# Two-layer hybrid mixer and mixture-of-experts kernel: normed rows stored from ScalarE's queue, routing reordered, one norm of four tiles between the layers

## The chip, the cores and the metric

The kernel runs on one core of one Trainium2 chip. The metric is the time of one execution on the device in microseconds (us); for a version it is the median of its runs. All times below are us unless marked otherwise. Engines are named TensorE (PE), VectorE (DVE), ScalarE (ACT), GpSimd (POOL) and SyncE (SP); SP does nothing but issue DMAs here.

## What is computed

Two layers, each a mixer of four kinds of heads and then a mixture of 16 experts with two experts per token, on 512 tokens of width 1024, all in fp32. Cut to what matters:

```python
for l in range(DEPTH):                                   # 2 layers
    sh1, sc1, g1, sh2, sc2, g2 = jnp.split(mod_all[l][:, None, :], 6, axis=-1)
    h = _rms_norm(x, norm_mix_g[l]) * (1.0 + sc1) + sh1
    proj = h @ w_in[l]
    ...
    mix = jnp.concatenate([y_nsa, y_pool, y_rwkv, y_dil], axis=-1).astype(x.dtype)
    x = x + g1 * (mix @ w_out[l])
    h2 = _rms_norm(x, norm_ffn_g[l]) * (1.0 + sc2) + sh2
    x = x + g2 * _moe(h2, router_w, router_b, moe_w_gate[l], moe_w_up[l], moe_w_down[l])

def _moe(h, router_w, router_b, w_gate, w_up, w_down):
    aff = jax.nn.sigmoid(jnp.einsum('bsd,de->bse', h, router_w).astype(F32))
    sel = (aff + router_b).reshape(B, S, N_EXPERT_GROUPS, EXPERTS_PER_GROUP)
    grp = jnp.argmax(jnp.sum(lax.top_k(sel, TOP_K)[0], axis=-1), axis=-1)
    ...                                                  # two experts of the best group, weights
    act = jax.nn.silu(hg) * hu * gates[..., None].astype(h.dtype)
    return jnp.einsum('bsef,efd->bsd', act, w_down)
```

## The kernel before

The 512 tokens are four tiles of 128 rows (`NT` = 4). Each layer goes through the same stages: the projection into the mixers (chunks of `w_in`, in the names `c` and `t`), the mixers themselves, the output projection `W_out`, the routing, and a loop over the 16 experts. Every large matmul is done as three (`mm3`, lines 616 to 618) on a high and a low part of each operand: ScalarE makes the high part of a weight (`wh`, line 568), VectorE the low part (`wl`, line 569). Weights come by DMAs of 512 KB that SP issues (line 585).

**What sets the order.** Each engine executes its instructions in the order in which they were emitted. The kernel emits them from Python generators: one main program and side streams, which `W.spawn` adds. At each `yield` a planner (`_Clock`, a model of every engine's time, and the weaver `W`) decides which stream emits next; it knows a cost for each instruction and the moment at which its data is ready by that model. A stream that yields a flag is resumed once the flag is done.

**The output projection and the routing** (lines 1836 to 2100). `W_out` is done in two halves of 512 columns. `evac(t, p_)` (line 1981) scales a tile of the result and adds it to `xt[t]` on VectorE, squares it on ScalarE (`jk`, line 1986), and for the second half writes x*A into `hs[t]` on GpSimd (line 1989) and spawns `norm(t)`. `half(t, q)` (line 1847) transposes four 128x128 blocks of tile t on TensorE (`tp`), copies them on ScalarE (`xT`, line 1853), multiplies them with the router (`lg`) and adds the result into `lgt`. `norm(t)` (line 1865) computes 1/rms of the rows (`rsl`) on VectorE, scales the tile, and stores it in DRAM as `h2d` (line 1884), from where the experts' rows are gathered later. By `NQ = "VVAV"` tile 2 is scaled on ScalarE with an addition on GpSimd, the others by two operations of 128x512 on VectorE (line 1882). After tile 2's store, `keep` (line 1888) stores the residual rows of tiles 0 to 2 (`xs_d`, or the output in the last layer) from ScalarE's queue (`XWQ` = 2).

`route` (line 1903) waits for all four tiles: logits times `rsl`, a tanh on ScalarE (`aff`, line 1911), scores (`sel`, `prs`), the best group (`gsc` and after), the two experts, and each token's rank within its expert (`rank`). `onehot(e)` (line 1895) writes eight one-hot matrices of 128x128 for experts e and e+1 on VectorE, `slots` (line 2048) turns them into row numbers (`idx`) by small matmuls on TensorE (`sps`), and `slot_weights` (line 2061) into the rows' weights (`wt`, by `swt`). `gather(e)` (line 2073) is an indirect DMA of GpSimd that brings an expert's rows out of `h2d`; `etrans(e)` transposes them on TensorE (`etp`), and ScalarE and VectorE split them (`eh`, `el`). Experts 0 to 3 get slots and weights ahead of the loop; those of experts 4 to 15 are a side stream, `more_slots` (line 2090), two experts per block.

**Between the layers** (lines 2291 to 2312) the four tiles are read back from `xs_d`; ScalarE squares them (`square`, line 822), and `normed_` normalises them by pairs (0, 1) and (2, 3), the even tile on ScalarE, the odd one on VectorE. Layer 1 then transposes the normed tiles (`tp`, line 906) in eight steps of `part_of` (line 912), each for 128 columns of all tiles: TensorE, then `hf`, `hH` and `hL` on ScalarE and VectorE. In layer 0 the upper four steps are a side stream for which `cchunk` waits at its third of four steps (line 984); in layer 1 all eight run first.

Of the kernel before, what the change touches and what calls it, by code (L numbers as in the profile page):

```python
# [36 lines left out]
ADG = ("c0","hdone","hdone")    # L37
ADL = 0  
ADE = "PPPPPPPP"
HWQ = 0  # L40
NQ = "VVAV"
SL = -1500  
PP = 1  
# [409 lines left out]
def fused(ctx: ExitStack, tc: tile.TileContext, A, out, dbg=None):  # L453
# [425 lines left out]
    def layer(l, xt, mixs, moes, nmixs):  # L879
# [32 lines left out]
        def part_of(ks, late=None):  # L912

            for k in ks:
                if l == 0:
                    src = f_ = hf[k // 2][:, k % 2]
                else:
                    src = transposed(k)
                    f_ = HG("hf1")
                if k % 2:  # L920
                    SC.activation(f_, src, AF.Identity, scale=A1[:, k:k + 1], bias=B1[:, k:k + 1])
                else:
                    V.tensor_scalar(f_, src, A1[:, k:k + 1], B1[:, k:k + 1], op0=OP.mult, op1=OP.add)
                SC.activation(parts[k][0], f_, AF.Copy)
                if late:
                    V.tensor_tensor(late[2], late[0], late[1].bitcast(F32), op=OP.subtract)  # L926
                late = (f_,) + parts[k]
                yield
            V.tensor_tensor(late[2], late[0], late[1].bitcast(F32), op=OP.subtract)

        upper = None
        if l == 0:
            def raise_(k):
                tp = transposed(k)
                if k % 2:
                    V.tensor_copy(hf[k // 2][:, k % 2], tp)
                else:
                    SC.activation(hf[k // 2][:, k % 2], tp, AF.Copy)

            def cols(jj):  # L940
                mcv = mcol(PB("mc"), 0, 4)
                hs_ = slice(4 * jj, 4 * jj + 4)
                V.scalar_tensor_tensor(A1[:, hs_], mcv[:, :, 2 + jj], 1.0, col("gmix", 4 * jj, 4), op0=OP.add, op1=OP.mult)
                V.tensor_copy(B1[:, hs_], mcv[:, :, jj])

            def upper_half():
                yield from ada_first(1)
                cols(1)
                yield
                yield from part_of(range(4, 8))  # L950

            ada_s.cap = 16
            ada_s.load(8)
            mixs.load(2)
            ada_s.load(12)
            mixs.load(3)
            ada_s.load(16)
            mixs.load(4)
            steps = ada_first(0)
            for _ in range(4):  # L960
                next(steps)
            for k in range(4):
                raise_(k)
            mixs.presplit(1)
            for _ in steps:
                pass
            cols(0)
            for k, _ in enumerate(part_of(range(4)), 4):
                raise_(k)
            upper = W.spawn(upper_half(), front=True, lead=0)  # L970
        else:
            for _ in part_of(range(8)):
                pass
        hH = [hH[k // 2][:, k % 2] for k in range(8)]
        hL = [hL[k // 2][:, k % 2] for k in range(8)]
        yield
# [865 lines left out]
        rank = lay.tile([128, 64], F32, name="rank")  # L1842
        mb = lay.tile([128, 64], BF, name="mb")
        hs = {}
        oh, hsides, normed = {}, {}, {}

        def half(t, q):

            xT_ = HG("xT")
            tp = PB("tp2")  # L1850
            for k in range(4):
                PE.transpose(tp[:, k * 128:(k + 1) * 128], xt[t][:, (4 * q + k) * 128:(4 * q + k + 1) * 128], ident)
            SC.activation(xT_, tp, AF.Copy)
            yield hsides.get((t, q - 1))
            lg = PB("lg")
            for k in range(4):
                PE.matmul(lg[:, 0:16], lhsT=xT_[:, k * 128:(k + 1) * 128], rhs=RP.rwa[:, 4 * q + k], start=k == 0,
                          stop=k == 3)
            ls_ = lgt[:, t * 16:(t + 1) * 16]
            if q:  # L1860
                V.tensor_tensor(ls_, ls_, lg[:, 0:16], op=OP.add)
            else:
                V.tensor_copy(ls_, lg[:, 0:16])

        def norm(t, after):

            ms, rs = TI("ms", 1), rsl[:, t:t + 1]
            V.tensor_scalar(ms, ms2[:, t, 0:1], ms2[:, t, 1:2], EPS, op0=OP.add, op1=OP.add)
            yield
            yield from rsqrt_cols(ms, rs, 1)  # L1870
            after.done, after.ready = True, K.mark
            if NQ[t] == "A":
                SC.activation(hs[t], hs[t], AF.Copy, scale=rs)
                yield
                for j in range(PP):
                    w_ = 1024 // PP
                    js = slice(j * w_, (j + 1) * w_)
                    GP.tensor_tensor(hs[t][:, js], hs[t][:, js], RP.B2.rearrange("p a b -> p (a b)")[:, js], op=OP.add)
            else:
                for j in range(2):  # L1880
                    js = slice(j * 512, (j + 1) * 512)
                    V.scalar_tensor_tensor(hs[t][:, js], hs[t][:, js], rs, RP.B2[:, j], op0=OP.mult, op1=OP.add)
                    yield
            HQ.dma_start(h2d[t * 128:(t + 1) * 128], hs[t])
            if XW == 0 and t == KP:
                keep(xt[:t + 1])
# [16 lines left out]
        def route():  # L1903
# [5 lines left out]
            yield  # L1909
            aff, sel = TI("aff"), TI("sel")  # L1910
            SC.activation(aff, lgt, AF.Tanh, scale=0.5)
            yield
            V.scalar_tensor_tensor(sel.rearrange("p (t e) -> p t e", t=4), aff.rearrange("p (t e) -> p t e", t=4),
                                   0.5, bc(RP.rb5[:, None, :], [128, 4, 16]), op0=OP.mult, op1=OP.add)
# [172 lines left out]
        slot_weights(0, 4)  # L2087
        SF = {e: _Flag() for e in range(4, NE, 2)}

        def more_slots():  # L2090
            for e in range(4, NE, 2):
                onehot(e, range(NT))
                yield
                slots(e, e + 2)
                slot_weights(e, e + 2)
                oh.pop(e)
                SF[e].done, SF[e].ready = True, K.mark
                yield
# [135 lines left out]
                                              in_=yo, in_offset=None, bounds_check=S - 1, oob_is_err=False,  # L2234
                                              compute_op=OP.add)

        W.spawn(more_slots())
        if XW == 2:
            keep(xt)
        etrans(0)  # L2240
# [48 lines left out]
        if last:  # L2289
            return  # L2290
        xt = load_x(xs_d)
        rsn_, ms = TI("rsn_", 4), TI("ms", 4)

        def normed_(ts):
            ms_ = ms[:, ts[0]:ts[-1] + 1]
            V.tensor_scalar(ms_, ms_, 1.0 / D, EPS, op0=OP.mult, op1=OP.add)
            for _ in rsqrt_cols(ms_, rsn_[:, ts[0]:ts[-1] + 1], len(ts)):
                pass
            for u in ts:
                x_ = G("xn")  # L2300
                if u % 2:
                    V.tensor_scalar(x_, xt[u], rsn_[:, u:u + 1], None, op0=OP.mult)
                else:
                    SC.activation(x_, xt[u], AF.Copy, scale=rsn_[:, u:u + 1])
                xn[u] = x_

        xn = {}
        for t in range(NT):
            square(xt[t], ms[:, t:t + 1])
            if t % 2:  # L2310
                normed_((t - 1, t))
        nxt.append([xn[t] for t in range(NT)])

    nxt = []

# [31 lines left out]
```

## Time and profile before

| | |
|---|---|
| median of 3 runs | 1262.56 us (1259.57 to 1263.63) |
| profiled execution, its own time | 1272.69 us |
| its span in the profile | 1270.9 us |
| mean granted clock of TensorE | 0.935 |
| busy: PE / DVE / ACT / POOL | 1106.8 / 874.7 / 581.7 / 167.6 us |
| share of the span | 87% / 69% / 46% / 13% |
| moved by DMA | 232.05 MB, mean 183 GB/s |

The profile is of one execution, and its times are counted from its start. Busy time of an engine is the time in which it executed something, so DMA issues, branches and semaphores are not in it. The output projection of layer 0 ends and its routing runs at about 415 to 454 us, its experts to about 640; layer 1's routing stands at about 1040 to 1077. A granted clock of 1.00 is TensorE at its full rate, 0.5 at half of it.

### The profile page before, as it was taken

The page shows a single profiled execution, that of the slowest core. Times are in us where ns is not written, and L with a number is a line of the kernel's source. Part 1 is how long each engine was busy: PE and PEld are TensorE (multiplying, and loading weights), DVE is VectorE, ACT ScalarE, POOL GpSimd, SP SyncE. Part 2 cuts the span into 40 slices and gives each one's busy share as a digit, 9 for nine tenths or more (in the row PEclk, how much of TensorE's full clock was granted, in tenths as well). Part 3 has the DMA queues.
Part 4 walks back from the last instruction along what each step waited for, and adds up shares of the span by engine and source line. Part 5 has one row for each costly group of instructions (what it writes and reads, how often), then busy time and mean ns, then how long its engine had stood idle before and what let it go on. Part 6 is the DMA issues. An engine that isn't in the chain of part 4 may idle for free. (4 is left out here: it accounts for less than half of the span.)

```text
span 1270.9 us, 21609 instructions
## 1 busy us (share of the span) xinstructions
PE 1106.8 (87%) x8158; PEld 822.9 (65%) x8158; DVE 874.7 (69%) x2208; ACT 581.7 (46%) x1076; POOL 167.6 (13%) x140
## 2 busy tenths in 40 slices
PE   4999999899899679999839979999888994999995
PEld 2677768545678456677628657775576783667774
DVE  4538686557654679999853466865775465999995
ACT  3443033336663255776543411243576531667762
POOL 2000000100001221244210000001000022213431
PEclk9999999969899889999969989999988996999998
DMA  9512001968141859999451121029321418699982
GB/s 350 198 51 84 35 21 55 361 210 318 33 159 65 312 216 324 316 371 352 154 194 38 34 83 35 22 87 406 125 92 46 170 56 345 237 327 344 352 292 37
DMA packets 68319, 232.05 MB, mean 183 GB/s; under 512 B 10580, under 2 KB 11460, under 8 KB 68208
## 3 DMA queue, kind: packets, MB, share of 16 engines
q1 hardware_dynamic: 54960, 192.18, 41.1%
q0 software_dynamic: 10368, 27.92, 7.9%
q10 hardware_dynamic: 2880, 10.49, 2.1%
q8 instruction: 67, 1.10, 0.3%
q14 instruction: 44, 0.36, 0.1%
HBM read 213.76 MB, written 25.17 MB: 188 GB/s over the span
## 5 line engine op out<-in xcount | busy, mean ns | idle before, releaser
L569 DVE TENSOR_TENSOR wl<-raw,wh 128x1024 fp32r<-128x1024 f32 (+2 forms) x254 | 300.4, 1199 | 43.9 <-ACT wh L568 40.7
L568 ACT ACTIVATE wh<-raw 128x1024 fp32r<-128x1024 f32 (+2 forms) x254 | 251.1, 1038 | 14.4 <-DMA raw<-w_out 8.7
L618 PE MATMUL gu<-wh,el 128*128 128x512 f32 x256 | 102.5, 400 | 2.3 <-DVE el L569 1.3
L616 PE MATMUL gu<-wh,eh 128*128 128x512 f32 x256 | 104.4, 408 | 0.0
L617 PE MATMUL gu<-wl,eh 128*128 128x512 f32 x256 | 101.0, 394 | 0.0
L568 ACT ACTIVATE eh<-etp 128x512 fp32r<-128x512 f32 x64 | 35.0, 595 | 112.7 <-PE etp L2107 112.6
L616 PE MATMUL t<-wh,hH 128*128 128x512 f32 (+1 forms) x192 | 79.1, 412 | 0.0
L617 PE MATMUL t<-wl,hH 128*128 128x512 f32 (+1 forms) x192 | 71.2, 371 | 6.1 <-DVE wl L569 6.1
L618 PE MATMUL c<-hH,wl 128*128 128x512 f32 x176 | 70.1, 398 | 3.0 <-DVE wl L569 3.0
L616 PE MATMUL c<-hH,wh 128*128 128x512 f32 x176 | 71.7, 407 | 0.9 <-ACT wh L568 0.9
L617 PE MATMUL c<-hL,wh 128*128 128x512 f32 x176 | 70.1, 398 | 2.0 <-DVE hL L926 2.0
L618 PE MATMUL t<-wh,hL 128*128 128x512 f32 (+1 forms) x192 | 70.5, 367 | 0.0
L1353 POOL TENSOR_SCALAR sd<-st,pcs 128x64 f32<-128x64 f32 x28 | 13.4, 491 | 413.2 <-DVE st L1377 315.5
L616 PE MATMUL dp<-wh,ahl 128*128 128x512 f32 x128 | 54.2, 424 | 15.1 <-ACT ahl L568 15.1
L618 PE MATMUL dp<-wh,ahl 128*128 128x512 f32 x128 | 54.2, 423 | 12.7 <-DVE ahl L569 12.7
L1678 ACT ACTIVATE P<-P,mx 128x128 f32<-128x128 f32 (+3 forms) x96 | 52.7, 551 | 27.1 <-DVE mx L1675 20.2
L618 PEld LDWEIGHTS gu<-wh,el 128*128 128x128 f32 x256 | 48.5, 190 | 17.6 <-DVE el L569 7.7
L2075 POOL DMA_INDIRECT ga<-h2d,idx x32 | 48.0, 1501 | 54.7 <-PE gu L617 17.1
L617 PEld LDWEIGHTS gu<-wl,eh 128*128 128x128 f32 x256 | 49.1, 192 | 9.3
L616 PEld LDWEIGHTS gu<-wh,eh 128*128 128x128 f32 x256 | 48.9, 191 | 9.0 <-ACT eh L568 0.5
L1697 PE MATMUL ptp<-cbase,P 128*128 128x128 f32 x240 | 44.2, 317 | 11.4 <-ACT pt L1699 5.2
L616 PE MATMUL wo<-wh,mH 128*128 128x512 f32 x128 | 52.4, 409 | 0.0
(597 smaller groups left out, 2388.9 us busy)
## 6 DMA issues: line engine op xcount, KB each, us to landing
raw<-w_gu SPq DMA_DIRECT2D x120, 512.0 KB, 8.0
raw<-ada_w SPq DMA_DIRECT2D x96, 512.0 KB, 7.8
raw<-w_dn SPq DMA_DIRECT2D x60, 512.0 KB, 7.7
raw<-win_c SPq DMA_DIRECT2D x16, 512.0 KB, 10.2
raw<-win_t SPq DMA_DIRECT2D x16, 512.0 KB, 3.2
raw<-w_out SPq DMA_DIRECT2D x16, 512.0 KB, 4.3
x<-x SPq DMA_DIRECT2D x8, 512.0 KB, 5.4
h2d<-h SPq DMA_DIRECT2D x8, 512.0 KB, 6.4
```

The lines of the kernel that those rows point to most:

```text
L568: SC.activation(h_, src, AF.Copy)
L569: eng.tensor_tensor(l_, src, h_.bitcast(F32), op=OP.subtract)
L616: PE.matmul(o, lhsT=sh, rhs=mh, start=first, stop=False)
L617: PE.matmul(o, lhsT=sh, rhs=ml, start=False, stop=False)
L618: PE.matmul(o, lhsT=sl, rhs=mh, start=False, stop=last)
L1353: GP.tensor_scalar(sd[:, i * 64:(i + 1) * 64], st[c][:, i * 64:(i + 1) * 64], pcs[i][:, c:c + 1], 0.0, op0=OP.mult, op1=OP.add)
L1678: SC.activation(P[:, par, :n], P[:, par, :n], AF.Exp, scale=-1.0, bias=mx[:, par:par + 1], accum_out=den[:, par:par + 1])
L1697: PE.transpose(tp[:, ks_], P[:, par, ks_], ident)
L2075: GP.indirect_dma_start(out=g_, out_offset=None, in_=h2d, in_offset=bass.IndirectOffsetOnAxis(ap=info[e][0], axis=0))
```

## The change

`HWQ` = 2 issues the `h2d` stores from ScalarE's queue instead of SP's. In `half`, a `yield` stands between the router's matmuls and the addition of their result. In `norm`, tile 3 is scaled only after `route` has emitted the tanh (the flag `tanhed`), without a `yield` between its two operations. `more_slots` takes a range: experts 4 to 7 are done at once before `etrans(0)`, experts 8 to 15 stay a side stream. Between the layers, `rms` (line 829, as at the start of layer 0: tiles 0 and 2 squared on ScalarE, 1 and 3 on VectorE, one reciprocal root of four columns) takes the place of the pairs. In layer 1 the upper four steps of `part_of` become a side stream as in layer 0.

```diff
--- before.py
+++ after.py
@@ -37,7 +37,7 @@
 ADG = ("c0","hdone","hdone")  
 ADL = 0  
 ADE = "PPPPPPPP"
-HWQ = 0
+HWQ = 2
 NQ = "VVAV"
 SL = -1500  
 PP = 1  
@@ -969,8 +969,9 @@
                 raise_(k)
             upper = W.spawn(upper_half(), front=True, lead=0)
         else:
-            for _ in part_of(range(8)):
+            for _ in part_of(range(4)):
                 pass
+            upper = W.spawn(part_of(range(4, 8)), front=True, lead=0)
         hH = [hH[k // 2][:, k % 2] for k in range(8)]
         hL = [hL[k // 2][:, k % 2] for k in range(8)]
         yield
@@ -1842,7 +1843,7 @@
         rank = lay.tile([128, 64], F32, name="rank")
         mb = lay.tile([128, 64], BF, name="mb")
         hs = {}
-        oh, hsides, normed = {}, {}, {}
+        oh, hsides, normed, tanhed = {}, {}, {}, _Flag()
 
         def half(t, q):
 
@@ -1856,6 +1857,7 @@
             for k in range(4):
                 PE.matmul(lg[:, 0:16], lhsT=xT_[:, k * 128:(k + 1) * 128], rhs=RP.rwa[:, 4 * q + k], start=k == 0,
                           stop=k == 3)
+            yield
             ls_ = lgt[:, t * 16:(t + 1) * 16]
             if q:
                 V.tensor_tensor(ls_, ls_, lg[:, 0:16], op=OP.add)
@@ -1877,10 +1879,13 @@
                     js = slice(j * w_, (j + 1) * w_)
                     GP.tensor_tensor(hs[t][:, js], hs[t][:, js], RP.B2.rearrange("p a b -> p (a b)")[:, js], op=OP.add)
             else:
+                if t == 3:
+                    yield tanhed
                 for j in range(2):
                     js = slice(j * 512, (j + 1) * 512)
                     V.scalar_tensor_tensor(hs[t][:, js], hs[t][:, js], rs, RP.B2[:, j], op0=OP.mult, op1=OP.add)
-                    yield
+                    if t < 3:
+                        yield
             HQ.dma_start(h2d[t * 128:(t + 1) * 128], hs[t])
             if XW == 0 and t == KP:
                 keep(xt[:t + 1])
@@ -1909,6 +1914,7 @@
             yield
             aff, sel = TI("aff"), TI("sel")
             SC.activation(aff, lgt, AF.Tanh, scale=0.5)
+            tanhed.done = True
             yield
             V.scalar_tensor_tensor(sel.rearrange("p (t e) -> p t e", t=4), aff.rearrange("p (t e) -> p t e", t=4),
                                    0.5, bc(RP.rb5[:, None, :], [128, 4, 16]), op0=OP.mult, op1=OP.add)
@@ -2087,8 +2093,8 @@
         slot_weights(0, 4)
         SF = {e: _Flag() for e in range(4, NE, 2)}
 
-        def more_slots():
-            for e in range(4, NE, 2):
+        def more_slots(e0, e1):
+            for e in range(e0, e1, 2):
                 onehot(e, range(NT))
                 yield
                 slots(e, e + 2)
@@ -2234,7 +2240,9 @@
                                               in_=yo, in_offset=None, bounds_check=S - 1, oob_is_err=False,
                                               compute_op=OP.add)
 
-        W.spawn(more_slots())
+        for _ in more_slots(4, 8):
+            pass
+        W.spawn(more_slots(8, NE))
         if XW == 2:
             keep(xt)
         etrans(0)
@@ -2289,27 +2297,16 @@
         if last:
             return
         xt = load_x(xs_d)
-        rsn_, ms = TI("rsn_", 4), TI("ms", 4)
-
-        def normed_(ts):
-            ms_ = ms[:, ts[0]:ts[-1] + 1]
-            V.tensor_scalar(ms_, ms_, 1.0 / D, EPS, op0=OP.mult, op1=OP.add)
-            for _ in rsqrt_cols(ms_, rsn_[:, ts[0]:ts[-1] + 1], len(ts)):
-                pass
-            for u in ts:
-                x_ = G("xn")
-                if u % 2:
-                    V.tensor_scalar(x_, xt[u], rsn_[:, u:u + 1], None, op0=OP.mult)
-                else:
-                    SC.activation(x_, xt[u], AF.Copy, scale=rsn_[:, u:u + 1])
-                xn[u] = x_
-
-        xn = {}
+        rsn_ = rms(xt)
+        xn = []
         for t in range(NT):
-            square(xt[t], ms[:, t:t + 1])
+            x_ = G("xn")
             if t % 2:
-                normed_((t - 1, t))
-        nxt.append([xn[t] for t in range(NT)])
+                V.tensor_scalar(x_, xt[t], rsn_[:, t:t + 1], None, op0=OP.mult)
+            else:
+                SC.activation(x_, xt[t], AF.Copy, scale=rsn_[:, t:t + 1])
+            xn.append(x_)
+        nxt.append(xn)
 
     nxt = []
 
```

What the planner makes of it is read from the order of the instructions on each engine. `h2d` are the stores of normed rows, `xs_d` those of the residual, `jk` squares, `xT` the transposed tiles for the router, `aff` the tanh; the numbers in the names tell buffers apart (`h_4012`, `h_4077`, `h_4161` and `h_4218` are tiles 0 to 3 after the change).

On ScalarE, at the end of layer 0's output projection and in its routing, before:

```order
L1853 ACTIVATE xT<-tp_4202 128x512
L1986 ACTIVATE jk,ms_3827<-x 128x512
L1853 ACTIVATE xT<-tp_4256 128x512
L1873 ACTIVATE h_4158<-h_4158,rsl 128x1024
L1986 ACTIVATE jk,ms_3827<-x 128x512
L1890 DMA xs_d<-x 128x1024 x3
L1853 ACTIVATE xT<-tp_4315 128x512
L2033 ACTIVATE g2s<-brow 128x512 x2
L1911 ACTIVATE aff<-lgt 128x64
L1890 DMA xs_d<-x 128x1024
```

and after:

```order
L1854 ACTIVATE xT<-tp_4227 128x512
L1854 ACTIVATE xT<-tp_4261 128x512
L1875 ACTIVATE h_4161<-h_4161,rsl 128x1024
L1889 DMA h2d_3824<-h_4077 128x1024
L1889 DMA h2d_3824<-h_4161 128x1024
L1895 DMA xs_d<-x 128x1024 x3
L1992 ACTIVATE jk,ms_3827<-x 128x512
L1854 ACTIVATE xT<-tp_4315 128x512
L2039 ACTIVATE g2s<-brow 128x512 x2
L1916 ACTIVATE aff<-lgt 128x64
L1889 DMA h2d_3824<-h_4218 128x1024
L1895 DMA xs_d<-x 128x1024
```

Tile 3's square and `xT` stood ahead of, or right behind, three `xs_d` stores; now two `h2d` stores and the three `xs_d` stores stand ahead of both, and tile 3's store behind the tanh. The second `h2d` store there waits for GpSimd's addition of tile 2; the third `xs_d` store for the semaphore that the store of tile 1 (`h_4077`) sets. Layer 1 has the same order, with the output in the place of `xs_d`.

On VectorE in layer 0's routing, from tile 3's scale on, before:

```order
L564 SCALAR_TENSOR_TENSOR rsl<-rq_t,rsl 128x1
L1882 SCALAR_TENSOR_TENSOR h_4225<-h_4225,rsl,B_3589 128x512 x2
L1906 TENSOR_TENSOR lgt<-lgt,rsl 128x64
L1908 TENSOR_TENSOR lgt<-lgt,rbias 128x64
L1913 SCALAR_TENSOR_TENSOR sel<-aff,rb_3414 128x64
L1919 TENSOR_TENSOR prs<-sel 128x16x3
L1921 TENSOR_TENSOR prs<-sel 128x16
L1926 TENSOR_REDUCE gsc<-prs 128x16
```

and after:

```order
L564 SCALAR_TENSOR_TENSOR rsl<-rq_t,rsl 128x1
L1911 TENSOR_TENSOR lgt<-lgt,rsl 128x64
L1913 TENSOR_TENSOR lgt<-lgt,rbias 128x64
L1919 SCALAR_TENSOR_TENSOR sel<-aff,rb_3414 128x64
L1925 TENSOR_TENSOR prs<-sel 128x16x3
L1927 TENSOR_TENSOR prs<-sel 128x16
L1886 SCALAR_TENSOR_TENSOR h_4218<-h_4218,rsl,B_3589 128x512 x2
L1932 TENSOR_REDUCE gsc<-prs 128x16
```

Tile 3's two scaling operations (128x512) have moved behind the scores `sel` and `prs`.

On VectorE between the slot weights of experts 0 to 3 and expert 0's `el`, one piece of the difference:

```order
L2075 TENSOR_REDUCE wt<-swt 128x4
L1903 TENSOR_SCALAR oh<-iob,rank 128x128 x8
L2065 TENSOR_TENSOR idx<-sps,ioff 128x4
L2075 TENSOR_REDUCE wt<-swt 128x2
L569 TENSOR_TENSOR el<-etp,eh 128x512 x2
```

The two blocks stand ahead of `el` now, and on TensorE their 32 `sps` and 16 `swt` matmuls ahead of expert 0's transposes `etp`. Between later experts two such blocks are gone.

On TensorE at the start of layer 1's projection, before:

```order
L906 MATMUL tp<-cbase,xn 128x128 x32
L616 MATMUL c_6854<-hH,wh 128x512
L617 MATMUL c_6854<-hL,wh 128x512
L618 MATMUL c_6854<-hH,wl 128x512
L616 MATMUL c_6854<-hH,wh 128x512
```

and after:

```order
L906 MATMUL tp<-cbase,xn 128x128 x20
L616 MATMUL c_6795<-hH,wh 128x512
L617 MATMUL c_6795<-hL,wh 128x512
L618 MATMUL c_6795<-hH,wl 128x512
L618 MATMUL c_6797<-hH,wl 128x512
L906 MATMUL tp<-cbase,xn 128x128 x4
L616 MATMUL c_6798<-hH,wh 128x512
```

Twenty transposes stand ahead of the first projection matmul instead of 32; the other twelve follow in three groups of four between projection matmuls. From layer 1's mixers to its output projection the side streams' instructions are dealt out in another order as well, without any added or removed; no row shows that shortly.

## Rows read from the trace of the kernel before

**Rows 1.** Windows: stretch, its us, busy us of each engine, PEclk, DMA share, GB/s.

```profile
430.00:454.00 24.00, 10.51 (x83) 6.71 (x81) 12.83 (x72) 3.05 (x7) 5.38 (x4) 0.64 0.92 362
...
480.00:520.00 40.00, 37.21 (x238) 28.21 (x238) 39.61 (x79) 24.53 (x34) 8.67 (x7) 1.00 0.95 329
...
40.00:370.00 330.00, 308.08 (x2759) 219.27 (x2751) 205.33 (x651) 133.21 (x311) 10.46 (x19) 0.93 0.37 132
...
663.00:1032.00 369.00, 341.96 (x2916) 255.88 (x2917) 224.37 (x670) 150.98 (x341) 11.40 (x21) 0.95 0.28 99
```

**Rows 2.** Waits of SP's queue, 411 to 470 us: line, releaser, total us, times, longest.

```profile
SPq L585 <- DMA xs_d<-x: 6.5, 2, 5.0
```

**Rows 3.** Timeline of ScalarE, layer 0's routing: start us, us, line, operation, [idle before].

```profile
428.47 1.15 ACT L1873 ACTIVATE h<-h,rsl 128x1024 f32<-128x1024 f32 x1 [3.02 <-DVE rsl L564]
...
429.85 0.83 ACTq L1890 DMA_DIRECT2D xs_d<-x  x2
...
431.26 0.60 ACT L1853 ACTIVATE xT<-tp 128x512 f32<-128x512 f32 x1 [0.74 <-issue]
...
436.83 0.25 ACT L1911 ACTIVATE aff<-lgt 128x64 f32<-128x64 f32 x1
```

**Rows 4.** Timeline of the same stretch, GpSimd and VectorE.

```profile
431.01 2.34 POOL L1878 TENSOR_TENSOR h<-h,B 128x1024 f32<-128x1024 f32 x1
...
434.88 1.41 DVE L1882 SCALAR_TENSOR_TENSOR h<-h,rsl,B 128x512 f32<-128x512 f32 x2
...
444.00 1.38 DVE L1898 TENSOR_SCALAR oh<-iob,rank 128x128 bf16<-128x128 bf16 x8
...
448.91 0.17 DVE L2069 TENSOR_REDUCE wt<-swt 128x4 f32<-128x12 f32 x1 [0.68 <-PE swt L2067]
```

**Rows 5.** Timeline of the same stretch, GpSimd's first gather and TensorE's first transposes.

```profile
447.63 1.05 POOL L2075 DMA_INDIRECT ga<-h2d,idx  x1 [14.28 <-DVE aff L1976]
...
452.07 1.94 PE L2107 MATMUL etp<-cbase,ga 128*128 128x128 f32 x8 [3.19 <-DMA ga<-h2d,idx]
```

**Rows 6.** Landing of h2d stores (line 1884's view), of gathers (line 2075's), of xs_d stores.

```profile
DMA to landing us min/median/max: 6.1/6.2/6.9
...
DMA to landing us min/median/max: 4.3/4.8/5.3
...
xs_d<-x ACTq DMA_DIRECT2D x4, 512.0 KB, 8.4
```

**Rows 7.** Timeline of ScalarE, the expert loop of layer 0: the silu of each step.

```profile
475.07 0.38 ACT L2125 ACTIVATE ac<-gu 128x256 f32<-128x256 f32 x1
...
486.70 0.39 ACT L2125 ACTIVATE ac<-gu 128x256 f32<-128x256 f32 x1
...
565.75 0.39 ACT L2125 ACTIVATE ac<-gu 128x256 f32<-128x256 f32 x1
...
576.51 0.39 ACT L2125 ACTIVATE ac<-gu 128x256 f32<-128x256 f32 x1
```

**Rows 8.** Loads between the layers (line 532's view); layer 0's norm; TensorE after the norm.

```profile
L532 SPq DMA_DIRECT2D x<-xs_d x4: 336/370/371, 642.9 to 644.3; - x4
...
DMA to landing us min/median/max: 3.2/5.1/7.0
...
12.01 1.22 DVE L833 CUSTOM_DVE_ANT_0 jk<-x 128x1024 f32<-128x1024 f32 x1
...
15.78 2.19 ACT L898 ACTIVATE x<-x,rs__168 128x1024 f32<-128x1024 f32 x2 [4.97 <-DVE rs__168 L547]
...
658.10 4.86 PE L906 MATMUL tp<-cbase,xn 128*128 128x128 f32 x26 [4.50 <-ACT xn L2304]
...
663.55 0.48 PE L616 MATMUL c<-hH,wh 128*128 128x512 f32 x1
```

**Rows 9.** Timeline of layer 1's routing: the weights' end and the first transposes.

```profile
1073.01 0.17 DVE L2069 TENSOR_REDUCE wt<-swt 128x4 f32<-128x12 f32 x1 [0.68 <-PE swt L2067]
...
1076.89 1.51 PE L2107 MATMUL etp<-cbase,ga 128*128 128x128 f32 x6 [3.91 <-DMA ga<-h2d,idx]
```

## Prediction, before the changed kernel was run

> **What bounds the kernel now.** I began with the table of windows. In most of the program TensorE is the limit, but not in the two places that the change touches. In the expert loop of layer 0, VectorE was busy 39.61 of 40 us [rows 1]: a step there is as long as VectorE's work. In the stretch just ahead, where the tokens are routed, TensorE did 10.51 us of work in 24, at a granted clock of 0.64, with the DMA engines 0.92 busy [rows 1]. That stretch is a chain of waits, and whatever lengthens the chain lengthens the kernel. The third place is the start of layer 1. There TensorE was busy 341.96 us of 369, so 27.0 us idle, where the same stage of layer 0 left 21.9 of 330 idle [rows 1].
>
> The chain of waits in routing is read from the timelines. Tile 3's xT copy on ScalarE stands behind three DMA issues, from 429.85 on, and starts at 431.26; the tanh (aff) follows at 436.83 [rows 3]. From there VectorE computes scores, ranks and one-hot rows, and its weights (wt) end at 449.08 [rows 4]. TensorE's first transposes of expert 0 start at 452.07, after 3.19 us of waiting for the gathered rows [rows 5]. So before the change, the rows bound the start of the experts; VectorE's chain was done 2.99 us earlier (452.07 - 449.08).
>
> The waits of SP's queue show something the code does not say. Two loads of weights on SP waited 6.5 us for the landing of xs_d stores, which no load depends on [rows 2]. So DMA instructions share their completion semaphores in turn: an issue can be held until an earlier, unrelated DMA has landed, and everything behind it in that engine's queue waits too. On SP only transfers stand behind. On ScalarE it is computation.
>
> **The change part by part.**
>
> *Stores from ScalarE's queue.* It removes four issues of h2d from SP in each layer and puts them on ScalarE; SP's own loads move up past them, which is worth nothing while the DMA engines are 0.92 busy [rows 1]. What counts is the order on ScalarE: h(2), store of tile 1, store of tile 2, three xs_d stores, and only then tile 3's square (jk) and xT. The third xs_d store waits for the semaphore of tile 1's store, which is issued right behind h(2). h(2) takes 1.15 us [rows 3]; ScalarE had waited 3.02 us for its scale, since 425.45 [rows 3], and the scale is now computed ahead of the last evacuation, so I put its start at 426.0. The store then goes out at about 427.2. The h2d stores landed in 6.1, 6.2 and 6.9 us (min, median, max) [rows 6]. It lands at 433.3 to 434.1; 0.4 for the held issue and 0.8 for the square with its read-out give xT at 434.5 to 435.3, where it was at 431.26 [rows 3]: +3.2 to +4.0. I take **+3.6**, since the stretch is the one in which those landings were measured. The lower bound is a store that is no wait at all: then tile 2's own store still waits for GpSimd's addition, 2.34 us from h(2)'s end [rows 4], to about 429.6, four issues of some 0.4 follow (0.83 for two [rows 3]), and xT comes at 432.1: +0.8. The upper bound takes 8.4 us, the median of the xs_d stores, which do come from ScalarE's queue [rows 6]: +5.5.
>
> Does the other queue make the landing shorter? xs_d from ScalarE took 8.4 us at the median in that stretch, h2d from SP 6.2 [rows 6]: nothing speaks for it. The Trainium skill, "DMA: Bandwidth & Descriptors", section "Issuing engines are not separate DMA queues", says that DMAs of the scalar, sync and gpsimd engines run on the same 16 DMA engines, and that several issuers save only the sequencer's time to start them. By that rule the store on ScalarE gains nothing and the sum stays as it is; were the emptier queue quick, and the store to land in the 4.3 us of the quickest gather of its size in the stretch [rows 6], the hold would be some 1.4 instead of 3.6 and the sum 4.4 lower. The 8.4 beside 6.2 agrees with the rule.
>
> *Tile 3's normed row waits for the tanh.* The two VectorE operations that make it take 1.41 us [rows 4]. Before, they stood ahead of the logits' scaling, at 434.88, beside TensorE's row broadcasts and ScalarE's copies, which the tanh had to wait for anyway; now they stand between the scores and the group maximum, on the chain: **+1.41** for VectorE, and nothing gained ahead, as the tanh waits behind the second copy on ScalarE. The row is also stored later: tanh's end near 440.7, 0.7 for scores, 1.41, so 442.9; landing 6.1 to 6.9 gives 449.8 at most. From the gather's start (447.63) to the transposes (452.07) it took 4.44 us [rows 5], so the rows would allow a start by 454.7. That is not late: the next part is later.
>
> *Two blocks of slots ahead of expert 0.* Experts 4 to 7 now get their one-hots, slots and weights before expert 0's transposes. A block is 8 one-hots (1.38 us [rows 4]), about 0.3 for the last of 16 small matmuls, 0.16 for idx, 0.3 for weights' matmuls and 0.17 for wt: 2.2 us, and 2.0 for the second, whose wt TensorE does not wait for. So TensorE reaches the transposes **4.3 us** after wt.
>
> Together in layer 0: 449.08 + 3.6 + 1.41 + 4.3 = 458.4 against 452.07, **+6.3 us**; what waited for the rows (3 us) is swallowed. The bounds with +0.8 and +5.5 are +3.5 and +8.2. Layer 1 has the same order with wt ending at 1073.18 and the transposes at 1076.89 [rows 9]: **+5.6**, from +2.8 to +7.5.
>
> *Two blocks fewer in the loop.* From 475.07 to 486.70, a step with a block, is 11.63 us; from 565.75 to 576.51, one without, 10.76 [rows 7]. Six steps of a layer hold a block now, four after the change: 2 x 0.9 = **-1.8 us per layer**. A saving of the whole VectorE time (1.8 per block) would be -3.6, and none at all 0.
>
> *Between the layers.* One norm of four tiles starts when the last has landed, 644.3 + 7.0 = 651.3 [rows 8]. VectorE squares it in 1.22; in layer 0, whose input has the same norm, 2.55 us later ScalarE began two tiles, 2.19 us [rows 8]. So 651.3 + 1.22 + 2.55 + 2.19 = 657.3, against 658.10 now [rows 8]: the early pair, done first today, hid nothing that counts. Then 20 transposes in place of 32 (4.86 us for 26, 0.187 each) let the first projection start at 661.0, not 663.55 [rows 8]: -2.5. But the other 12 now stand in the projection: +2.2. **-0.3**, from -2.5 (they fall into gaps) to +1.9 (each group of four stalls for its own length again).
>
> *The order of layer 1's side streams.* The planner, seeing other costs, deals its mixers out differently from there to the output projection. The trace has no row for an order that was not run. Nearest are the idle times of the two layers' own orders, 21.9 and 27.0 us [rows 1]: I take **0** and hold 5 us either way open.
>
> **The sum.** 6.3 + 5.6 - 3.6 - 0.3 = **+8.0 us**. The profiled execution took 1272.69 us (span 1270.9), 10.1 above the median of the three runs, 1262.56; the stretches above are short and the differences carry over. So the profile would be 1280.7 and the median **1270.6 us**. The ends without the order are 3.5 + 2.8 - 7.2 - 2.5 = -3.4 and 8.2 + 7.5 + 1.9 = +17.6. A difference of 0.3%, 3.8 us, is what a measurement of this kernel can tell.
>
> **The rivals.**
>
> *ScalarE is not held.* Tile 1's store lands before the third xs_d store's turn, hold 0.8 in each layer: 3.5 + 2.8 - 3.6 - 0.3 = +2.4, **1265.0 us**. For it: a transfer of that size landed in 4.3 us [rows 6], and h(2), so the store behind it, may run earlier than I put it. Against: loads on SP did wait that long for stores [rows 2]. Chance 0.19, most of it within 0.3%.
>
> *The start of layer 1 fills up, and the kernel is faster.* The projection starts 2.5 us earlier with its transposes in gaps, and the streams behind it idle no more than layer 0's: 5.1 us less [rows 1]. That is -7.6 where I have -0.3, and with the forecast's routing +0.7, 1263.3. It decides the sign only where the holds on ScalarE are under about 1.3 us; with 0.8 each the sum is -4.9, **1257.7 us**. For it: 27.0 us idle with weights on hand (DMA share 0.28 there [rows 1]). Against: an order may as well idle more, and both must hold. Chance 0.18, with other gains in that stage counted in.
>
> *It goes worse on both counts.* Landings of 8.4 us in both layers, since the DMA engines are busier with loads that SP issues earlier, and layer 1's order loses 5: 8.2 + 7.5 - 3.6 - 0.3 + 5 = +16.8, **1279.4 us**. Chance 0.08.
>
> **How the numbers follow.** My forecast keeps 0.55; of that 0.50 is slower by over 0.3%, 0.05 within. With the rivals (0.14 of the first within and 0.05 slower; of the second 0.17 faster, 0.01 within; the third slower): slower 0.63, within 0.3% 0.20, faster 0.17. Range **1257 to 1279 us**: from the second rival's time to the third's, with about a tenth beyond each end. The forecast's own range is 1264 to 1277.
>
> **What would show it.** In layer 0 of the changed kernel's profile: ScalarE's queue waiting at an xs_d store for a DMA h2d; xT of tile 3 near 434.9; tanh near 440.4; wt near 454; the first etp near 458.4, with no wait for the gathered rows, behind three swt groups. In the loop: four steps of 11.6 us where there were six, the others 10.75. Between the layers: xn done near 657.3 and the first c matmul near 661, from the profile's own zero and less the shift of routing. I am wrong if xT of tile 3 starts before 432.5 (the store's semaphore is not what holds ScalarE), if etp still waits for the gather (the stores then land late), or if the stretch from the first c matmul to the output projection changes by more than 5 us.

## The result and the profile after

The changed kernel took 1275.86 us (median of 5 runs, 1271.60 to 1278.62), the kernel before 1262.56 (5 runs, 1259.37 to 1263.63): a ratio of **1.0111, 95% interval 1.0079 to 1.0143**, 13.3 us slower. The profiled execution of the changed kernel took 1274.98 us (span 1273.1, granted clock 0.935). That is only 2.3 above the profiled execution of before, because that one lay 10.1 above its median; the two profiles can't be compared as wholes, so they are cut into stages below.

ScalarE's timeline in layer 0's routing answers to [rows 3] (start us, us, line, operation, idle before it and what ended that):

```profile
419.09 1.15 ACT L1875 ACTIVATE h<-h,rsl 128x1024 f32<-128x1024 f32 x1 [0.19 <-DVE rsl L564]
419.12 3.94 ACTq L1889 DMA_DIRECT2D h2d<-h  x2
423.09 4.09 ACTq L1895 DMA_DIRECT2D xs_d<-x  x3
427.29 0.60 ACT L1992 ACTIVATE jk<-x 128x512 f32<-128x512 f32 x1 [7.04 <-DMA h2d<-h]
...
427.92 0.58 ACT L1854 ACTIVATE xT<-tp 128x512 f32<-128x512 f32 x1
...
434.57 0.25 ACT L1916 ACTIVATE aff<-lgt 128x64 f32<-128x64 f32 x1
```

Between tile 2's scaling (h(2), the first line) and tile 3's square (jk) ScalarE stood still for 7.04 us, and what let it go was the landing of an h2d store. The tile had been ready since 423.25, when VectorE's evacuation ended. Of the three xs_d issues, the third is the one that waited (the same timeline from 424.4 us on):

```profile
426.86 0.33 ACTq L1895 DMA_DIRECT2D xs_d<-x  x1
```

The second had ended at 424.27, and the semaphore of tile 1's store, issued at 419.12, was full at 426.84: 2.6 us of the delay are this landing. The rest comes before it: tile 2's store waited until 422.71 for GpSimd's addition, and the issues behind it follow one another. Layer 1 shows the same idle time, to 0.01 us:

```profile
1048.27 3.93 ACTq L1889 DMA_DIRECT2D h2d<-h  x2
1052.24 4.08 ACTq L1895 DMA_DIRECT2D out_dram<-x  x3
1056.42 0.60 ACT L1992 ACTIVATE jk<-x 128x512 f32<-128x512 f32 x1 [7.03 <-DMA h2d<-h]
```

The rest of layer 0's routing, to compare with [rows 4, 5], from the timelines of VectorE, GpSimd and TensorE:

```profile
435.44 1.41 DVE L1886 SCALAR_TENSOR_TENSOR h<-h,rsl,B 128x512 f32<-128x512 f32 x2
436.76 0.25 DVE L1932 TENSOR_REDUCE gsc<-prs 128x16 f32<-128x96 f32 x1
...
442.19 1.06 POOL L2081 DMA_INDIRECT ga<-h2d,idx  x1 [17.60 <-DVE oh L1903]
...
448.25 0.17 DVE L2075 TENSOR_REDUCE wt<-swt 128x4 f32<-128x12 f32 x1 [0.68 <-PE swt L2073]
448.34 1.38 DVE L1903 TENSOR_SCALAR oh<-iob,rank 128x128 bf16<-128x128 bf16 x8
...
451.84 0.35 PE L2073 MATMUL swt<-dtw,oh 128*128 128x3 bf16 x8
452.05 1.95 PE L2113 MATMUL etp<-cbase,ga 128*128 128x128 f32 x8
```

Tile 3's scaling stands on the chain ahead of gsc; the two blocks stand between wt and etp (448.25 to 452.05, 3.8 us from wt's start, 3.6 from its end); and etp has no wait for gathered rows any more. Between the layers, beside [rows 8]:

```profile
640.71 1.76 SPq L532 DMA_DIRECT2D x<-xs_d  x4
...
653.13 2.19 ACT L2307 ACTIVATE xn<-x,rs__6716 128x1024 f32<-128x1024 f32 x2 [3.88 <-DVE rs__6716 L547]
...
655.37 4.10 PE L906 MATMUL tp<-cbase,xn 128*128 128x128 f32 x18 [0.35 <-ACT xn L2307]
659.12 0.78 PE L616 MATMUL c<-hH,wh 128*128 128x512 f32 x1
...
663.63 0.60 PE L906 MATMUL tp<-cbase,xn 128*128 128x128 f32 x4
```

The first c matmul comes 18.4 us after the x loads' first issue (20.6 before); a group of four transposes stands in the projection and takes 0.35 us of TensorE's stream (663.63 to 663.98).

### The profile page after: what moved, and what is told of

It is laid out like the page before. It is cut to its first block, busy times and chain, and to the rows that moved or that the text cites. A ratio compares the mean times of both kernels' runs of the same rounds, so it can differ in the third digit from the quotient of the medians.

```text
span 1273.1 us, 21586 instructions
## 1 busy us (share of the span) xinstructions
PE 1105.0 (87%) x8158; PEld 821.7 (65%) x8158; DVE 880.9 (69%) x2191; ACT 578.8 (45%) x1068; POOL 174.0 (14%) x140
## 5 line engine op out<-in xcount | busy, mean ns | idle before, releaser
L617 PE MATMUL dp<-wl,ahl 128*128 128x512 f32 x128 | 50.9, 398 | 0.0
```

The lines of the kernel that those rows point to most:

```text
L617: PE.matmul(o, lhsT=sh, rhs=ml, start=False, stop=False)
```

## Experiments

Ten runs were made: nine edited kernels, and the kernel before once more. Each edited kernel ran 12 times, and its ratio is to the kernel before on the same occasion (23 to 35 runs, medians 1262.24 to 1263.16). Each profile was cut at the same events of TensorE (first and last matmul of a kind; "x loads" is their first issue on SP, "end" the last matmul), read from its timelines. "wo" are the output projection's matmuls, c and t those of the projection into the mixers, etp the transposes of expert 0's rows. Lengths in us:

| kernel | to first wo, L0 | last wo to etp, L0 | etp to x loads | to first c, L1 | c stage | to last t | to first wo, L1 | wo stage, L1 | last wo to etp, L1 | etp to end |
|---|---|---|---|---|---|---|---|---|---|---|
| before | 373.6 | 24.0 | 190.9 | 20.6 | 77.6 | 122.3 | 134.4 | 54.5 | 24.6 | 181.9 |
| before, again | 367.2 | 24.0 | 192.2 | 20.7 | 77.6 | 122.1 | 128.3 | 54.5 | 24.5 | 181.7 |
| before, stores on ScalarE | 363.3 | 28.3 | 190.6 | 20.7 | 77.6 | 122.3 | 128.3 | 54.5 | 26.6 | 181.7 |
| changed | 367.1 | 30.5 | 188.7 | 18.4 | 77.8 | 126.0 | 133.2 | 55.6 | 29.3 | 180.1 |
| changed, stores on SP | 368.1 | 27.0 | 188.9 | 18.6 | 77.7 | 127.5 | 135.1 | 55.6 | 25.6 | 179.9 |
| changed, xs_d on SP | 368.7 | 26.5 | 189.0 | 16.7 | 79.4 | 123.3 | 136.3 | 55.5 | 26.5 | 180.1 |
| changed, other order | 368.6 | 30.9 | 188.6 | 18.2 | 77.8 | 124.1 | 129.0 | 54.4 | 30.6 | 179.8 |
| changed, blocks as side | 366.8 | 26.5 | 191.5 | 18.3 | 78.1 | 124.2 | 129.1 | 54.4 | 27.0 | 181.9 |
| the same, stores on SP | 369.4 | 23.9 | 189.1 | 16.8 | 79.4 | 121.4 | 134.5 | 55.4 | 23.9 | 181.9 |
| before, joint norm | 365.3 | 24.7 | 190.6 | 17.4 | 81.1 | 121.4 | 128.1 | 54.5 | 24.6 | 181.9 |
| the same, one block | 364.3 | 25.0 | 188.4 | 18.2 | 79.0 | 122.3 | 130.3 | 54.5 | 24.8 | 181.0 |
| the same, xs_d on SP | 364.8 | 23.8 | 189.1 | 18.1 | 77.8 | 124.1 | 130.2 | 54.5 | 23.8 | 181.1 |

### The kernel before, once more

> The kernel before once more, for a second profile. The profile of before was 10.1 us above the median of its runs, and its stage ahead of layer 0's output projection (the same instructions in both kernels) took 373.6 us where the changed kernel took 367.1. If that is chance of one execution, this profile has the stage near 367 and a span near 1261, and the other stages as before: 24.0 from the last wo matmul to etp in layer 0. If it belongs to the kernel, the stage is near 373 again.

One execution, 1261.35 us, span 1259.3. The stage ahead of layer 0's output projection was 367.2, and layer 1's last mixers 128.3 where the first profile had 134.4, with the same instructions; the routings agree within 0.2. So the 10 us of the first profile lay in the mixers and were chance. The windows of layer 1's last mixers in the two executions (stretch, us, busy us of PE, PEld, DVE, ACT, POOL, PEclk, DMA share, GB/s), the first profile's:

```profile
863.00:998.00 135.00, 119.22 (x1100) 82.24 (x1100) 87.31 (x345) 77.17 (x219) 5.69 (x14) 0.90 0.44 163
```

and the second's:

```profile
858.00:987.00 129.00, 115.00 (x1101) 80.14 (x1100) 87.30 (x346) 77.47 (x220) 5.57 (x14) 0.91 0.46 168
```

VectorE and ScalarE were busy as long; TensorE needed 4.2 us more for the same matmuls. A single profile can't be trusted to 6 us in a mixer stage. The routings agree as wholes because the gathered rows end both: inside, the tanh came 5.6 us behind xT in the first profile of layer 0 and 6.7 in the second. In the second, tile 3's router matmuls (lg) took 1.89 us at a granted clock of 0.50 (1.2 GHz), in the first 1.07 at 1.00 (2.4 GHz), behind the same work.

### The stores back on SP

```diff
-HWQ = 2
+HWQ = 0
```

> The changed kernel with the h2d stores back on SP's queue; TensorE's and VectorE's order stays what the change made it. Theory (ScalarE is held): tile 3's square no longer waits 7.0 us for a landing, xT of tile 3 follows the last evacuation by about 1.2 us instead of 4.7, and TensorE is not cold for the router's matmuls: 3.5 to 4.5 us less in each layer, so 1267 to 1269 us. Rival (the added blocks of slots and the tanh wait cost the time, the queue is beside it): within 1.5 us of the changed kernel, 1275.9. Rival (layer 1's order costs it): also no change.

1268.02 us, ratio to the kernel before 1.0038 (1.0013 to 1.0063): of the 13.3 us, 7.8 are gone. ScalarE in layer 0:

```profile
420.49 1.15 ACT L1875 ACTIVATE h<-h,rsl 128x1024 f32<-128x1024 f32 x1 [0.65 <-DVE rsl L564]
420.52 1.88 ACTq L1895 DMA_DIRECT2D xs_d<-x  x3
424.71 0.60 ACT L1992 ACTIVATE jk<-x 128x512 f32<-128x512 f32 x1 [3.07 <-DVE lgt L1863]
...
425.37 0.60 ACT L1854 ACTIVATE xT<-tp 128x512 f32<-128x512 f32 x1
```

The three xs_d issues take 1.88 us where they took 4.09; xT starts 0.74 us after the end of VectorE's last evacuation (layer 1: 0.75), in the changed kernel 4.67 and 3.93. The routings are 3.5 and 3.7 us shorter, as the theory had it for the hold. The clock did not follow in both layers: tile 3's lg still took 1.89 us in layer 0 and 1.06 in layer 1, against 1.89 in both in the changed kernel.

### The residual stores on SP, the h2d stores on ScalarE

```diff
-XWQ = 2
+XWQ = 0
```

> The changed kernel with the residual stores (xs_d, and the output in layer 1) on SP instead of ScalarE; the h2d stores stay on ScalarE, TensorE's and VectorE's order stays the same. Theory (it is the xs_d store's wait for the landing of tile 1's store that holds ScalarE): the hold goes though the h2d stores stay, 3.5 us less in each layer, 1268 to 1269. Rival (issuing the h2d stores on ScalarE costs it by itself): 1274 to 1277. The residual's loads on SP may be held by these stores; then the loop starts later by that.

1269.85 us, ratio 1.0056 (1.0028 to 1.0084). ScalarE still issues two h2d stores there, and tile 3 isn't held:

```profile
420.77 3.94 ACTq L1889 DMA_DIRECT2D h2d<-h  x2
424.99 0.60 ACT L1992 ACTIVATE jk<-x 128x512 f32<-128x512 f32 x1 [3.09 <-DVE lgt L1863]
...
425.65 0.60 ACT L1854 ACTIVATE xT<-tp 128x512 f32<-128x512 f32 x1
```

xT follows the evacuation by 0.76. The routings are 4.0 and 2.8 us shorter; the median lies 0.9 above the theory's range and far from the rival's. So it is neither the issue of h2d nor of xs_d by itself, but the two on one compute engine, where a later store waits for an earlier one's landing.

### The queue alone, in the kernel before

```diff
-HWQ = 0
+HWQ = 2
```

> The kernel before with nothing changed but the queue of the h2d stores (ScalarE); TensorE's and VectorE's order is the same row by row. Theory: an xs_d store on ScalarE again stands behind a store's semaphore, ahead of xT of tile 3; 3 to 4.5 us more in each layer, 1268.5 to 1271.5. Rival (stores off SP are free of SP's waits and the gathers start sooner; here etp waits for the gathered rows): up to 3 us less in each layer, 1256.5 to 1262.5.

1264.40 us, ratio 1.0032 (1.0012 to 1.0053): about 4 us slower by the ratio, 2.0 by the medians (1262.43 beside it), and less than forecast. ScalarE is held, but not as the theory had it:

```profile
420.75 2.33 POOL L1878 TENSOR_TENSOR h<-h,B 128x1024 f32<-128x1024 f32 x1
423.12 0.33 ACTq L1884 DMA_DIRECT2D h2d<-h  x1
423.49 1.90 ACTq L1890 DMA_DIRECT2D xs_d<-x  x3
425.44 0.60 ACT L1853 ACTIVATE xT<-tp 128x512 f32<-128x512 f32 x1 [5.18 <-issue]
...
446.12 1.95 PE L2107 MATMUL etp<-cbase,ga 128*128 128x128 f32 x8
```

Tile 2's store goes out at 423.12, when GpSimd's addition has ended (423.08); three xs_d issues follow without a wait of their own, since tile 1's store had landed by 423.31, before the second of them started. So no xs_d store waited for a landing here: the hold is the wait of tile 2's store for GpSimd, and the issues behind it. xT comes 6.0 us after the evacuation (1.6 before; layer 1: 5.6), but the routing grew by only 4.3 and 2.1: etp no longer waits for gathered rows. The rival was half right: the rows do come in time, and part of the hold is paid with that wait.

### Layer 1's order

```diff
             upper = W.spawn(part_of(range(4, 8)), front=True, lead=0)
+            K.free["PE"] = K.pe + 600
```

> The changed kernel, but the planner is told once, at the start of layer 1's projection, that TensorE is 0.6 us later than it thinks; routing, loops and norms keep their instructions, and only the order in which layer 1's mixers are dealt out goes back to near the kernel before's (36 rows of TensorE apart instead of 321). Theory (that order costs time by itself): the stage from the last c matmul to the last t matmul goes from 126 back to 122 to 124 us, the output projection from 55.6 to 54.4, and the total falls by 6 to 9: 1267 to 1270. Rival (the stages are longer because of the side stream and the joint norm): no change, 1274.5 to 1277.

1270.52 us, ratio 1.0070 (1.0047 to 1.0094): 5.3 us of the 13.3 belong to the order, just short of the 6 to 9 expected. The changed kernel has only five runs, so the 5.3 is known to some 4 us either way. The windows of layer 1's last mixers, changed kernel:

```profile
863.00:996.00 133.00, 118.71 (x1080) 78.88 (x1074) 85.57 (x335) 76.53 (x217) 4.83 (x12) 0.87 0.46 167
996.00:1052.00 56.00, 54.98 (x279) 45.74 (x276) 33.33 (x67) 19.95 (x33) 11.76 (x8) 0.97 0.38 131
```

and with the other order:

```profile
863.00:992.00 129.00, 113.39 (x1093) 77.94 (x1092) 86.66 (x344) 77.06 (x220) 4.85 (x13) 0.93 0.46 167
992.00:1046.00 54.00, 53.26 (x276) 44.64 (x274) 33.40 (x66) 19.75 (x32) 10.12 (x8) 1.00 0.37 129
```

The granted clock is 0.93 for 0.87 in the mixers and 1.00 for 0.97 in the output projection; TensorE's work is the same. The three profiles with the changed kernel's order have 133.2, 135.1 and 136.3 us in that stage; but other orders had 134.4 and 134.5 once each, so one profile does not prove it. Over the whole stretch from the first c matmul to the output projection (c stage, to last t, to first wo) the three have 337.0, 340.3 and 339.0 us, and the nine with orders near the kernel before's 328.0 to 335.3. Which part of the order costs the time, and why the clock is lower with it, stays open.

### The blocks of slots back in the side stream

```diff
-        for _ in more_slots(4, 8):
-            pass
-        W.spawn(more_slots(8, NE))
+        W.spawn(more_slots(4, NE))
```

> The changed kernel with experts 4 to 7's slots again in the side stream. Theory: etp of expert 0 starts when wt is done, 3.8 us earlier in each layer than with the two blocks ahead, and the loop takes back 1.8: 2 us less per layer, so about 1272 us. Rival (the blocks are free there, since TensorE would wait for the gathered rows): no change in the start of etp, and 1.8 us more per layer in the loop, about 1279.5. Layer 1's mixers are dealt out in another order again, so the stages are compared by themselves too.

1265.04 us, ratio 1.0018 (0.9991 to 1.0045), 10.8 less than the changed kernel, where 4 was expected. Layer 1's order came out 6 rows of TensorE from that of the last run, the other order, so that is the pair to compare: 1270.52 to 1265.04, 5.5 us. By stages etp comes 4.4 and 3.6 us sooner and the loops are 2.9 and 2.0 longer: 3.1. The stages bear the theory out; the 2.4 left are within what such medians scatter.

### And the stores on SP as well

> The changed kernel with the h2d stores on SP and all later slots in the side stream; left are the tanh wait, the yield, the joint norm and the side stream. Theory: without the hold and without the blocks the routing is as long as before, since the gathered rows bound it: 24 us from the last wo matmul to etp in layer 0 and 24.5 in layer 1; with the -2.2 between the layers 1260 to 1261. Rival (the tanh wait delays the last store and so the gather by 2 us or more): 26 us, 1264 to 1265.

(The last edit and the first.) 1261.22 us, ratio 1.0003 (0.9973 to 1.0032). The routings are 23.9 us, and rows bind again:

```profile
448.95 1.94 PE L2113 MATMUL etp<-cbase,ga 128*128 128x128 f32 x8 [2.63 <-DMA ga<-h2d,idx]
```

Tanh wait, yield, joint norm and side stream are left in it, and it is as fast as the kernel before, to within 0.3%.

### The part between the layers alone

(In the kernel before: `rms(xt)` for the pairs, `part_of(range(4))` and the spawned upper half.)

> The kernel before with the change's part between the layers alone: one norm of four tiles, upper half of h as a side stream (layer 1's order 67 rows from the kernel before's). Theory: the first c matmul comes 2.2 us sooner after the x loads (18.4 for 20.7) and the twelve transposes cost nothing in the c stage: 1260.3. Rival (the transposes in the c stage take it back): 1262 to 1263. Rival (a side stream in layer 1 makes the order bad): over 1266.

1259.25 us, ratio 0.9980 (0.9949 to 1.0012): 1.0 below the value expected, but the interval holds no change too. In this profile the first c comes 3.3 us sooner and the c stage is 3.5 longer; in all others with this part the two together are 95.8 to 97.3, against 98.2 before.

### One block ahead, not two

```diff
-        W.spawn(more_slots())
+        for _ in more_slots(4, 6):
+            pass
+        W.spawn(more_slots(6, NE))
```

(On the kernel of the run before this one; `more_slots` takes a range, as in the change. Layer 1's order is the same.)

> The kernel before with the joint norm and layer 1's side stream (as the run before with that part alone, same order in layer 1) and one block of slots, experts 4 and 5, ahead of expert 0 instead of the change's two. Theory: TensorE waits 2.5 to 3.9 us for the gathered rows between wt and etp, so a block of 2.2 us there is free, and one step fewer holds a block: 1.0 to 1.4 us less per layer, 1256.5 to 1257.5 with 1259.3 for that part alone; from the last wo matmul to etp 24.0 to 24.7 as before. Rival (the block delays etp all the same, since VectorE's el stands behind it): 1259 to 1261.

1256.73 us, ratio **0.9958 (0.9934 to 0.9982)**: faster than both kernels. The block lies where TensorE waited:

```profile
442.78 0.35 PE L2068 MATMUL swt<-dtw,oh 128*128 128x3 bf16 x8
443.74 1.94 PE L2108 MATMUL etp<-cbase,ga 128*128 128x128 f32 x8 [0.61 <-DMA ga<-h2d,idx]
```

0.61 us of the wait are left (2.55 without the block), and the loops are 2.2 and 0.9 shorter. The step from 1259.25 to 1256.73 is not clear of noise by itself; the stages bear it out.

> The same with the residual stores on SP, so that no DMA issue stands on ScalarE in the routing. Theory: xT of tile 3 loses its 0.7 to 1.1 us behind three issues, and the routing is 0.7 shorter in each layer: 1255 to 1256.5. Rival (SP's weight loads and h2d stores then wait behind the residual stores, so the gathered rows come later): 1258 to 1264.

With `XWQ = 0` on top: 1258.57 us, ratio 0.9974 (0.9948 to 1.0001). The routings are 1.2 and 1.0 us shorter in the profile, but the median isn't: it lies in the rival's range, 1.8 above the last run and within the noise of the two. The rival's reason is not seen (etp waits 0.73 and 0.59 us for the rows, 0.61 and 0.86 in the last run); inconclusive.

## Why the prediction came out as it did

The direction held, and the time lay in the range, 5.3 us above the forecast. Of the three signs of being wrong, the third came true (last point below). Step by step:

- **ScalarE held, +3.6 a layer: right, and shown.** xT came 3.1 and 2.4 us later behind the evacuation than before, 3.9 and 3.2 later than with the stores on SP. The store went out sooner than I put it (beside h(2)'s start, not behind its end) and landed later, 7.7 us after its issue (419.12 to 426.84); the two errors cancel, which is luck. 2.6 us are the landing; the rest is what the prediction kept as its lower bound, the wait for GpSimd's addition and the issues. The rival of no hold is refuted. The two profiles reach this place at different times, so the forecast's 434.9 and the sign's 432.5 are counted from the end of the last wo matmul: 6.9 and 4.5 us. Measured were 6.4.
- **Tanh wait, +1.41: right where the chain binds.** From aff to wt 13.7 us in both layers, 12.1 in the first profile of before (12.4 and 12.7 in the second). But without hold and blocks it costs nothing, as the gathered rows bind.
- **Blocks, 4.3 us after wt: 3.6** in each layer, from wt's end as the sum counts; a block takes 2.0, and the prediction's own 2.2 and 2.0 make 4.2.
- **TensorE's clock, not in the sum: +1.1 and +0.9.** From xT to the tanh it took 6.7 and 6.4 us, where the first profile of before had 5.6 and 5.5: tile 3's lg, behind a wait of 4.6 us for xT (1.5 before), ran at a granted clock of 0.50 and took 1.89 us for 1.07. The kernel before does so in some executions too, but there the wait for the rows takes it up.
- **The routing as a whole: right, in part by cancelling.** It was forecast +6.3 and +5.6 and measured +6.5 and +4.7 (24.0 to 30.5, 24.55 to 29.25, the mean of the two profiles of before). In layer 0 hold and blocks came out 0.5 and 0.7 below their terms, and the clock and the tanh wait 1.1 and 0.2 above.
- **Loops, -1.8 a layer: -2.9 and -1.7.** 191.5 to 188.7 and 181.8 to 180.1, means of before again. As forecast, two steps fewer are long, and those without a block take 10.75.
- **Between the layers, -0.3: -2.1.** Mis-sized: the twelve transposes were charged 2.2 us in the c stage, and the stage grew by 0.15. They take TensorE's time, but c has slack there; my bound of -2.5 was the nearer value.
- **Order of layer 1, 0: this is the step that failed.** "I take 0 and hold 5 us either way open": it cost 5.3 by the medians of two kernels that differ in the order alone. The idle times of the two layers' orders that I took as neighbours were the wrong quantity. From the first c matmul to the output projection TensorE was idle for 27.6 to 29.1 us in the three profiles with the changed kernel's order and 25.0 to 29.6 in the nine others; it was busy for 309.2 to 311.4 us against 302.4 to 308.3, at a granted clock of 0.93 to 0.94 against 0.94 to 0.96. So the cost shows as slower matmuls, not as idle time. That stretch grew by 2.7 us against the first profile of before and by 9.0 against the second; the sign of being wrong was 5. A change of 0.6 us in the planner's idea of TensorE's time, in one place, gives either order.

By medians the 13.3 us fall apart so: order 5.3, blocks 5.5, stores 3.8 (1265.04 to 1261.22; 7.8 with the blocks still there), the rest -1.3. The 3.8 by itself is not clear of noise. That 8.0, the forecast itself, is left beside the order is luck too: by the stages routing, loops and the part between the layers come to +4.5, and layer 1's mixers and output projection to some +6.8, so the order may weigh more than 5.3. The second rival had the first c sooner, as it said; the lower idle time it needed behind that did not come.

The Trainium skill, "DMA: Bandwidth & Descriptors", section "Issuing engines are not separate DMA queues", which the prediction weighed, says that DMAs run on the same DMA engines whichever engine issues them. The landings agree: ScalarE's queue made them no shorter. Tile 1's store took 7.7 us in the changed kernel, and 6.8 and 8.0 in the two layers with the residual stores on SP, where SP's took 6.1 to 6.9 [rows 6]. Tile 0's, issued ten us earlier, took 3.0 and 3.4 there, but one from SP took 2.7 in the run with the stores on SP and all later slots in the side stream. That the kernel with the other queue alone is 1.0032 times as long follows from the hold and says nothing of the queues.

## What to carry to other kernels

A DMA issued by an engine that computes can hold that engine for the landing of a transfer it has nothing to do with (2.6 us here), or for another engine that makes the stored data (GpSimd, in the kernel before with the other queue); read the order of the issues on such an engine for both before moving one there. Work moved ahead of a wait is free only up to the length of the wait: one block of 2.0 us fitted into 2.6, two lengthened the routings by 3.1 and 1.6 (the stores on SP, with and without them). Where a planner orders instructions, compare the order everywhere, and try the change with the order of a far stage nudged before crediting or blaming an edit.

## What was not expected

Eight router matmuls (lg) of tile 3 took 1.07 us in one execution of the kernel before and 1.89 in the next, with no instruction changed, at granted clocks of 1.00 and 0.50; a stage of identical instructions ahead of the first output projection took 363.3 to 373.6 us over these profiles. Runs of the kernel before reached from 1252.1 to 1272.0 us in the later comparisons. So differences of 2 or 3 us here are at the edge of what a dozen runs tell (the intervals above reach 0.2 to 0.3% to either side), and need stages to go with them.
